# First modulation block of a hybrid NSA and mLSTM trunk: shift and scale as columns straight from the weights, with small loads and masks moved

## Chip, core and metric

The kernel is written for one core of a Trainium2 chip and runs on that core alone. Its time is device microseconds (us) from one launch; lower is better. Before the change the median of three runs is 444.39 us (444.29 to 444.74).

## What is computed

Two layers stand behind each other, each modulated by a condition vector c. The part that matters here is the modulation at the head of layer 0:

```python
for i in range(DEPTH):
    shift, scale, gate = jnp.split(c @ ada_w[i] + ada_b[i], 3, axis=-1)
    h = rmsnorm(x, norm_g[i]) * (1.0 + scale[:, None, :]) + shift[:, None, :]
    y = nsa_mixer(h, ...) if i % 2 == 0 else mlstm_mixer(h, ...)
    x = x + gate[:, None, :] * y
return rmsnorm(x, final_g)
```

x is 256 x 1024 and c is 1 x 1024, all float32. Each mixer begins with the product h @ w_in over the 1024 channels. Shift and scale of one block of 128 channels are therefore two products of c (1024) with 1024 x 128 slices of `ada_w`.

## The kernel before

**Staging.** The 1024 channels are eight blocks of 128, counted by kk. Layer 0's first phase (`first_phase`, L391) loops over kk. For each block it needs the transposed, normalized x (`xT[:, kk]`), the shift and scale columns of that block (`cols`, 128 x 2), the modulated block `hh` with its rest `hl`, and the rows of `w_in` split into a rounded part `wh` (ScalarE, L163) and a rest `wl` (VectorE, L168). Each block then takes 42 matmuls of 256 columns (`proj`, L464 to L475) into seven PSUM banks. All of layer 0 is written in the order in which it runs on every engine (`manual_schedule`, L386): each engine works through its list, and only semaphores hold it.

**Opening, in the order of the code.** SyncE issues the two halves of x and then the stream of weights (`raw`, L87): two `ada_w` slices of 512 KB for block 0, block 0's `w_in` rows, and so on. ScalarE's queue issues c, `norm_g` and part of `ada_b` into `prc` (L257 to L259). TensorE runs nine dummy matmuls on a zero tile (`warm(9)`, L266), transposes `prc` (L396), and runs six more dummies (L397). VectorE copies the result into `pca` (L399), so that column k of `pca` is block k of c, and spreads c into `crep` (L401), 32 equal columns for each block. ScalarE sums the squares of x (L410). The reciprocal root is a chain of small operations on VectorE (L209 to L213), after which x is scaled in two pieces for each half: VectorE does half 1 (L413) and ScalarE does half 0 (L414), first 128 channels and then 896. TensorE transposes xn through PSUM (L455), 16 transposes in all.

**Shift and scale of block 0.** `ada_rows` (L216 to L228) keeps `crep` stationary, 32 columns at a time in four column groups of the array, and streams the raw weights through it: 16 matmuls for the shift and 16 for the scale. What comes out are partial rows; they are copied from PSUM to SBUF (L486 on VectorE, L488 on ScalarE) and turned into columns by a product with the selector `sel` (L441). VectorE adds the biases (L445, L443), and `hh[:, 0]` follows (L493). Block 1 does its `ada_rows` among the projections of block 0, at matmul 23, copies both rows at once (L543), transposes them at matmul 33 and sums them (`ada_sums`, L1669 to L1676). Later blocks use other code.

**GpSimd** in the opening makes constants: the identity, `sel` (a memset and four rows), `int1` and `intm`, distances (`dm`, `dc`; L291 to L302), and a mask (L305 to L311). Between these stand the five DMAs of `first_small` (L478), which load parameters for the end of the first phase (`parameters`, L458).

Of the kernel before, what the change touches and what calls it, by code (L numbers as in the profile page):

```python
# [11 lines left out]
AF = mybir.ActivationFunctionType  # L12
OP = mybir.AluOpType
AX = mybir.AxisListType

P = 128
SEQ = 256
D = 1024
# [5 lines left out]
class Kernel:  # L24
# [224 lines left out]
    def setup(self):  # L249
# [6 lines left out]
        prc = self.T(self.p1, [32, P])  # L256
        nc.scalar.dma_start(prc[0:8], row(t["c"][0]))  # L257
        nc.scalar.dma_start(prc[8:16], row(t["norm_g"][0]))
        nc.scalar.dma_start(prc[16:32], row(t["ada_b"][0, 0:2048]))  # L259
        for a in range(2):  # L260
            nc.sync.dma_start(self.x[:, a], xr[:, a])
        g = nc.gpsimd

# [22 lines left out]
        self.intm = self.T(pc, [P, 8], I32)  # L286
        g.memset(self.int1, 1)
        g.memset(self.intm, 0x7FFFFFFF)

# [13 lines left out]

        m32 = self.T(self.p1, [P, P])
        g.memset(m32, 0.0)  # L305
        g.affine_select(m32, m32, pattern=[[1, P]], compare_op=OP.is_ge, fill=-1e30, base=0, channel_multiplier=-1)
# [3 lines left out]
        g.tensor_copy(self.mask, m32)  # L310
        g.tensor_copy(self.identb, self.ident)  # L311
        nc.vector.tensor_copy(self.selh, self.ident[:, 32:40])
# [3 lines left out]

        self.prc, self.pra, self.prb = prc, pra, prb

    def small_loads(self):
# [23 lines left out]
    def layer1(self):  # L343
# [11 lines left out]
        for kk in range(KC):  # L355
            if kk > 1:
                self.pairs_stream(kk)
            else:
                self.cols_stream(0, kk, P)
# [31 lines left out]
    def first_phase(self, place):  # L391
# [4 lines left out]
        nc.tensor.transpose(bt[:, 0:32], self.prc, ident[:32, :32])  # L396
        self.warm(6)  # L397
        pca = self.pca = self.T(pc, [P, 96])
# [40 lines left out]

        def column0(bank, A, cols, b):  # L440
            nc.tensor.matmul(bank[:, b : b + 1], A, self.sel[:, 0:1], start=True, stop=True, skip_group_check=True)  # L441
            if b:
                nc.vector.scalar_tensor_tensor(cols[:, 1:2], bank[:, 1:2], pca[:, 24:25], pca[:, 8:9], op0=OP.add, op1=OP.mult)  # L443
            else:
                nc.vector.tensor_tensor(cols[:, 0:1], bank[:, 0:1], pca[:, 16:17], op=OP.add)  # L445

# [3 lines left out]
        def transposed(kc, n, b):  # L450

            b = b.rearrange("p (k m) -> p k m", k=n)
            for k in range(n):
                for a in range(2):
                    nc.tensor.transpose(b[:, k, a * P : a * P + P], xn[a][:, (kc + k) * P : (kc + k) * P + P], ident)  # L455
            return xT[:, kc : kc + n], b
# [19 lines left out]

        for dst, src in self.first_small:
            nc.gpsimd.dma_start(dst, src)  # L478
        halves, raws = [self.bank(7), self.bank(3)], self.take_raw(2)
        A0 = [self.T(pc, [P, 512], tag="adaA", bufs=2)[:, :P] for _ in range(2)]  # L480
# [5 lines left out]
        nc.vector.tensor_copy(A0[0], halves[0][:, 0:P])  # L486
# [6 lines left out]
        nc.vector.tensor_scalar(self.hh[:, 0], xT[:, 0], cols[:, 1:2], cols[:, 0:1], op0=OP.mult, op1=OP.add)  # L493
        h32 = self.T(p1, [P, SEQ], tag="y32", bufs=2)
        nc.scalar.activation(h32, xT[:, 0], AF.Identity, bias=cols[:, 0:1], scale=cols[:, 1:2])
        self.make_lo(*parts)
        rest(0, h32)
        copies.append(transposed(3, 2, self.bank(5)))
        copies.append(transposed(6, 2, self.bank(7)))
        copies.append(transposed(5, 1, b6[:, SEQ:]))  # L500
        self.guests_in = True
        for n in range(2):
            nc.scalar.activation(*copies[n], AF.Copy)
        nc.vector.tensor_copy(*copies[3])
        wide = self.make_hi(place[0][1])
# [3 lines left out]
        for kk in range(KC):  # L509

            if not kk:
                self.make_lo(*wide)
            ahead = 0 < kk < KC - 1
            if ahead:
# [22 lines left out]
            for n, _ in enumerate(proj(kk)):  # L537
                if (kk, n) == (7, 8):
                    parameters()
                if not kk and n == 23:  # L540
                    bank, raws = self.bank(7), self.take_raw(2)
                    self.ada_rows(bank, raws, SEQ)
                    nc.vector.tensor_copy(A1[:, :SEQ], bank[:, :SEQ])  # L543
                if not kk and n == 33:
                    cols = self.ada_sums(A1, 9, 17, 25, 0, 7, "cols", 1)
                    modulate(1, self.hh[:, 1], cols)
                    self.make_lo(*parts)
                elif 0 < kk < KC - 1 and n == 29:
                    cols = columns(kk + 1, A)
                    modulate(kk + 1, self.hh[:, kk + 1], cols)  # L550
                    self.make_lo(*parts)
                elif (kk, n) == (KC - 1, 17):
                    self.KH, self.KL = [self.T(p1, [P, 4, 512], F32R, tag=tag) for tag in ("KH", "KL")]
                    self.dup_split((self.KH, self.KL), 0, acc[6])
                    for dst, src in self.small:
                        nc.gpsimd.dma_start(dst, src)
                    self.E, self.F = [], {}
                    self.evac_cmp(acc[4])
                    self.hi_next()
                    self.evac_cmp(acc[5], True)  # L560
                    self.lo_next()
# [118 lines left out]
    def attention(self, hidden_block):  # L680
# [46 lines left out]
        def second():  # L727
# [7 lines left out]
            nc.gpsimd.memset(W["Kc"], 0.0)  # L735
            nc.gpsimd.memset(W["Vc"], 0.0)

        def ckeys():
# [960 lines left out]
```

## Time and profile before

| | |
|---|---|
| median of three runs | 444.39 us (444.29 to 444.74) |
| profiled execution: its own time | 446.02 us |
| profiled execution: span from first to last instruction | 444.2 us |
| TensorE busy (matmuls) | 433.4 us, 98% of the span |
| VectorE, ScalarE, GpSimd busy | 337.7, 277.0, 45.0 us |
| mean DMA rate over the span | 213 GB/s |
| TensorE busy in the first 30 us | 25.69 us |
| TensorE busy from 30 to 60 us | 30.00 us |

Times in the profile count from the span's start. PE is TensorE's matmuls, PEld its weight loads, DVE is VectorE, ACT ScalarE, POOL GpSimd and SP SyncE; a letter q behind an engine means its sequencer, which issues DMAs and waits. A row of the chain of waits gives start, duration and what ran then. A row of a stage gives its length, the busy time of each engine, the granted clock of TensorE as a share of full speed, the busy share of the DMA engines, and GB/s. A row of a line or a group ends in durations in nanoseconds. A matmul's duration holds its whole way through the array; how fast such instructions follow each other is read from the chain.

### The profile page before, as it was taken

Reading aid. Unit: us, or ns where it says so; the run is one execution under the profiler, and the core shown is the slowest. Engines: PE = TensorE matmul, PEld = TensorE weight load, DVE = VectorE, ACT = ScalarE, POOL = GpSimd, SP = SyncE. Lnnn points to the kernel's source line nnn. Section 1 sums busy time; section 2 is a strip of 40 time slices with the busy share of each in tenths; the row PEclk is TensorE's granted clock in tenths of the full one; section 3 lists DMA queues with packets and bytes.
Section 4 is the critical chain, followed back from the end, with each engine's and each line's share of the span. In section 5 each row is a group of like instructions: output and inputs, shape, how many; then the busy total and the mean of one; then the engine's idle time right before and its main releaser. Section 6 shows DMA issues by size and latency. Waiting matters only on the chain.

```text
span 444.2 us, 8146 instructions
## 1 busy us (share of the span) xinstructions
PE 433.4 (98%) x2938; PEld 372.8 (84%) x2938; DVE 337.7 (76%) x771; ACT 277.0 (62%) x553; POOL 45.0 (10%) x109
## 2 busy tenths in 40 slices
PE   6999999999999999999999999999999999999994
PEld 2999999798777877788899899988888888888884
DVE  4588989888786858697996489689986978548554
ACT  4566686767896795377748686464664555465522
POOL 8000052205205020012000000000000000000000
PEclk9899999999999999999999999999999999999998
DMA  8999969892299899998999999897845899840002
GB/s 282 373 361 357 388 211 263 211 374 87 69 299 346 196 236 341 226 190 173 263 120 91 152 342 240 166 167 235 252 149 171 213 193 275 267 143 0 1 1 94
DMA packets 73688, 94.58 MB, mean 213 GB/s; under 512 B 3800, under 2 KB 51008, under 8 KB 73648
## 3 DMA queue, kind: packets, MB, share of 16 engines
q1 hardware_dynamic: 72608, 92.29, 77.5%
q0 software_dynamic: 688, 0.97, 0.8%
q10 hardware_dynamic: 352, 0.80, 0.7%
q8 instruction: 23, 0.38, 0.3%
q14 instruction: 17, 0.14, 0.1%
HBM read 93.00 MB, written 1.05 MB: 212 GB/s over the span
## 4 chain that ended last, share of the span: by engine, by line
PE 94%; DVE 2%; DMA 1%; ACT 1%; issue 1%; ACTq 0%; DVEq 0%
PE bank L604 10%; PE bank L602 9%; PE bank L603 9%; PE bank L474 8%; PE bank L1652 6%; PE bank L1651 6%; PE bank L1650 6%; PE bank L926 5%; PE bank L1561 5%; PE bank L1091 5%; PE bank L1205 4%; PE bank L225 3%; PE bank L878 3%; PE bank L861 3%; PE bank L1441 2%; PE bank L818 2%
## 5 line engine op out<-in xcount | busy, mean ns | idle before, releaser
L168 DVE TENSOR_TENSOR wl<-raw,wh 128x1024 fp32r<-128x1024 f32 (+3 forms) x126 | 137.8, 1107 | 39.8 <-ACT wh L163 38.1
L163 ACT ACTIVATE wh<-raw 128x1024 fp32r<-128x1024 f32 (+3 forms) x126 | 118.5, 963 | 61.5 <-PE bank L604 28.5
L602 PE MATMUL bank<-wh,one 128*128 128x512 f32 (+1 forms) x208 | 76.8, 370 | 0.0
L603 PE MATMUL bank<-wl,one 128*128 128x512 f32 (+1 forms) x208 | 76.3, 367 | 0.0
L604 PE MATMUL bank<-wh,one 128*128 128x512 f32 (+1 forms) x208 | 76.3, 368 | 0.0
L1650 PE MATMUL bank<-one,wh 128*128 128x256 f32 x208 | 59.5, 286 | 0.0
L1652 PE MATMUL bank<-one,wl 128*128 128x256 f32 x208 | 59.2, 285 | 0.1
L1651 PE MATMUL bank<-one,wh 128*128 128x256 f32 x208 | 59.0, 284 | 0.0
L602 PEld LDWEIGHTS bank<-wh,one 128*128 128x128 f32 x208 | 39.2, 189 | 6.1 <-DVE tz L574 0.2
L604 PEld LDWEIGHTS bank<-wh,one 128*128 128x128 f32 x208 | 39.2, 188 | 6.1
L603 PEld LDWEIGHTS bank<-wl,one 128*128 128x128 f32 x208 | 39.2, 189 | 5.9
L1652 PEld LDWEIGHTS bank<-one,wl 128*128 128x128 f32 x208 | 39.7, 191 | 0.5 <-DVE wl L168 0.3
L1651 PEld LDWEIGHTS bank<-one,wh 128*128 128x128 f32 x208 | 39.8, 191 | 0.1
L1650 PEld LDWEIGHTS bank<-one,wh 128*128 128x128 f32 x208 | 39.7, 191 | 0.1
L474 PE MATMUL bank<-one,wh 128*128 128x256 f32 x224 | 31.7, 286 | 0.3 <-ACT one L438 0.3
L842 ACT ACTIVATE Pr<-Pr,mn 128x128 f32<-128x128 f32 (+1 forms) x64 | 28.2, 447 | 1.9 <-DVE mn L835 1.6
L474 PEld LDWEIGHTS bank<-one,wh 128*128 128x128 f32 x224 | 28.5, 191 | 0.8 <-ACT one L438 0.5
L856 POOL TENSOR_SCALAR Pr<-Pr,f 128x128 f32<-128x128 f32 (+1 forms) x24 | 18.9, 800 | 49.2 <-DVE f L850 34.8
L1422 DVE SCALAR_TENSOR_TENSOR conv<-bank,one,conv 128x255 f32<-128x255 f32 (+2 forms) x48 | 20.2, 472 | 2.1 <-ACT conv L1417 2.1
L835 DVE CUSTOM_DVE_ANT_0 Pr<-bank,one 128x128 f32<-128x128 f32 (+1 forms) x64 | 18.8, 351 | 3.2 <-PE bank L821 2.1
L686 ACT ACTIVATE PT<-bank 128x384 f32<-128x384 f32 x32 | 14.6, 487 | 8.3 <-PE bank L861 8.1
L926 PE MATMUL bank<-wh,Q 128*128 128x512 f32 x48 | 16.7, 405 | 0.0
(363 smaller groups left out, 815.1 us busy)
## 6 DMA issues: line engine op xcount, KB each, us to landing
raw<-in_b_w_in SPq DMA_DIRECT2D x62, 512.0 KB, 8.4
raw<-in_ada_w SPq DMA_DIRECT2D x34, 512.0 KB, 7.3
raw<-in_b_w_out SPq DMA_DIRECT2D x16, 512.0 KB, 4.4
raw<-in_a_w_in SPq DMA_DIRECT2D x8, 512.0 KB, 7.0
raw<-in_a_cmp_w SPq DMA_DIRECT2D x8, 512.0 KB, 4.5
raw<-in_a_w_in SPq DMA_DIRECT2D x16, 256.0 KB, 4.5
raw<-in_a_w_out SPq DMA_DIRECT2D x16, 256.0 KB, 6.6
raw<-in_a_w_in SPq DMA_DIRECT2D x8, 408.0 KB, 8.4
```

The costliest lines, as they stand in the source:

```text
L163: self.nc.scalar.activation(v(hi), src, AF.Copy)
L168: self.nc.vector.tensor_sub(v(lo), src, v(hi).bitcast(F32))
L474: nc.tensor.matmul(out, w[:, ch * P : ch * P + P], h[:, kk], start=(kk == 0 and m == 0 and ch % 2 == 0), stop=(kk == 7 and m == 2), skip_g ...
L602: nc.tensor.matmul(out, self.hh[:, kk, sl], wh, start=first, stop=False, skip_group_check=True)
L603: nc.tensor.matmul(out, self.hh[:, kk, sl], wl, start=False, stop=False, skip_group_check=True)
L604: nc.tensor.matmul(out, self.hl[:, kk, sl], wh, start=False, stop=last, skip_group_check=True)
L842: nc.scalar.activation(v, v, AF.Exp, bias=mn[:, a, br, j : j + 1], scale=-1.0, accum_out=sm[:, a, br, j : j + 1])
L926: nc.tensor.matmul(out, l[:, sl], w[:, c0:c1], start=(k == 0 and m == 0), stop=(k == 7 and m == 2), skip_group_check=True)
L1091: ins = nc.tensor.matmul(out, l[:, sl], w[:, c0:c1], start=(k == 0 and m == 0), stop=(k == N - 1 and m == 2), skip_group_check=True)
L1650: nc.tensor.matmul(out, wh, self.hh[:, kk], start=first, stop=False, skip_group_check=skip)
L1651: nc.tensor.matmul(out, wh, self.hl[:, kk], start=False, stop=False, skip_group_check=skip)
L1652: nc.tensor.matmul(out, wl, self.hh[:, kk], start=False, stop=last, skip_group_check=skip)
```

## The change

Block 0's shift and scale are computed as columns at once. For each of the two, eight products of one column accumulate in PSUM: a raw 128 x 128 piece of `ada_w` is the stationary operand and column kc of `pca` is what streams. The SBUF copies and the selector products for block 0 are gone, and so are 16 + 16 matmuls with `crep`. The eight products of the shift and the first four of the scale now stand ahead of the first pair of transposes, the last four behind it. The two `ada_w` slices come in five DMAs (two halves; a half and two quarters).

Beside that: c, `norm_g` and `ada_b` are issued by SyncE behind x; six dummy matmuls become three; `sel` is made on VectorE; `int1`, `intm`, the mask and the bf16 identity are made by GpSimd in the middle of layer 0 (`late_constants`); the five DMAs of `first_small` are issued by SyncE, emitted with block 2's step; the copies of the transposes are spread differently (L503 to L506 before). For block 1, `ada_rows` moves from matmul 23 to 27, its rows are copied by two engines, and the columns come from `sel` products at matmul 34.

```diff
@@ setup
-        nc.scalar.dma_start(prc[0:8], row(t["c"][0]))
-        nc.scalar.dma_start(prc[8:16], row(t["norm_g"][0]))
-        nc.scalar.dma_start(prc[16:32], row(t["ada_b"][0, 0:2048]))
         for a in range(2):
             nc.sync.dma_start(self.x[:, a], xr[:, a])
+        nc.sync.dma_start(prc[0:8], row(t["c"][0]))
+        nc.sync.dma_start(prc[8:16], row(t["norm_g"][0]))
+        nc.sync.dma_start(prc[16:32], row(t["ada_b"][0, 0:2048]))
...
-        g.memset(self.sel, 0.0)
+        nc.vector.memset(self.sel, 0.0)
         for j in range(4):
-            g.memset(self.sel[32 * j : 32 * j + 1], 1.0)
+            nc.vector.memset(self.sel[32 * j : 32 * j + 1], 1.0)
...
+    def late_constants(self):
+        g = self.nc.gpsimd
+        g.memset(self.int1, 1)
+        g.memset(self.intm, 0x7FFFFFFF)
+        m32 = self.T(self.p1, [P, P])
+        g.memset(m32, 0.0)
+        g.affine_select(m32, m32, pattern=[[1, P]], compare_op=OP.is_ge, fill=-1e30, base=0, channel_multiplier=-1)
+        g.tensor_copy(self.mask, m32)
+        g.tensor_copy(self.identb, self.ident)
@@ layer1
+                for b, cuts in enumerate(((0, 4, 8), (0, 4, 6, 8))):
+                    self.add(None, [P, KC, P], *[((lambda v, ks=slice(*ks): v[:, ks]), ada[:, ks[0] : ks[1], D * b : D * b + P]) for ks in zip(cuts, cuts[1:])])
@@ first_phase
-        self.warm(6)
+        self.warm(3)
...
+        def direct(b, ks):
+            for kc in ks:
+                nc.tensor.matmul(ones[b][:, b : b + 1], raws[b][:, kc], pca[:, kc : kc + 1], start=(kc == 0), stop=(kc == KC - 1), skip_group_check=True)
...
-        for dst, src in self.first_small:
-            nc.gpsimd.dma_start(dst, src)
-        self.ada_rows(halves[0][:, 0:P], raws, P, (0,))
+        direct(0, range(KC))
+        direct(1, range(4))
         b6 = self.bank(6)
         nc.vector.tensor_copy(*transposed(0, 1, b6[:, 0:SEQ]))
-        nc.vector.tensor_copy(A0[0], halves[0][:, 0:P])
-        self.ada_rows(halves[1], raws, SEQ, (1,))
-        nc.scalar.activation(A0[1], halves[1][:, P:SEQ], AF.Copy)
-        copies = [transposed(1, 2, self.bank(4))]
+        direct(1, range(4, KC))
         for b in range(2):
-            column0(ones[b], A0[b], cols, b)
+            column(ones[b], cols, b, 0)
+        nc.vector.tensor_scalar(self.hh[:, 0], xT[:, 0], cols[:, 1:2], cols[:, 0:1], op0=OP.mult, op1=OP.add)
+        copies = [transposed(1, 2, self.bank(4)), transposed(3, 2, self.bank(5)), transposed(6, 2, self.bank(7)), transposed(5, 1, b6[:, SEQ:])]
+        nc.scalar.activation(*copies[0], AF.Copy)
+        nc.vector.tensor_copy(*copies[1])
...
+            if kk == 2:
+                for dst, src in self.first_small:
+                    nc.sync.dma_start(dst, src)
...
-                if not kk and n == 23:
+                if not kk and n == 27:
                     bank, raws = self.bank(7), self.take_raw(2)
                     self.ada_rows(bank, raws, SEQ)
-                    nc.vector.tensor_copy(A1[:, :SEQ], bank[:, :SEQ])
-                if not kk and n == 33:
-                    cols = self.ada_sums(A1, 9, 17, 25, 0, 7, "cols", 1)
+                    nc.vector.tensor_copy(A1[:, P:SEQ], bank[:, P:SEQ])
+                    nc.scalar.activation(A1[:, 0:P], bank[:, 0:P], AF.Copy)
+                if not kk and n == 34:
+                    cols, bank = self.T(pc, [P, 2], tag="cols", bufs=4), self.bank(7)
+                    for b in (1, 0):
+                        nc.tensor.matmul(bank[:, b : b + 1], A1[:, b * P : b * P + P], self.sel[:, 0:1], start=True, stop=True, skip_group_check=True)
```

On TensorE, between the dummies (L247) and the projections, this stood before; KH and KL are the scaled halves of x, `raw` a slice of `ada_w`, and the last pair is the selector product:

```order
L247 MATMUL bank_165<-y_9_76 128x512
L225 MATMUL bank_203<-raw_205,one_58_174 32x128 x8
L455 MATMUL bank_244<-one_20_94,KH_180 128x128
L455 MATMUL bank_244<-one_20_94,KL_181 128x128
L225 MATMUL bank_204<-raw_207,one_58_174 32x128 x8
L455 MATMUL bank_258<-one_20_94,KH_180 128x128
L455 MATMUL bank_258<-one_20_94,KL_181 128x128
L455 MATMUL bank_258<-one_20_94,KH_180 128x128
L455 MATMUL bank_258<-one_20_94,KL_181 128x128
L441 MATMUL bank_234<-one_22_99,adaA_231 128x1
L441 MATMUL bank_235<-one_22_99,adaA_232 128x1
```

and this stands there now:

```order
L247 MATMUL bank_156<-y_9_76 128x512
L449 MATMUL bank_216<-one_54_160,raw_186 128x1 x8
L449 MATMUL bank_217<-one_54_160,raw_189 128x1 x4
L465 MATMUL bank_230<-one_20_94,KH_168 128x128
L465 MATMUL bank_230<-one_20_94,KL_169 128x128
L449 MATMUL bank_217<-one_54_160,raw_189 128x1 x4
L465 MATMUL bank_241<-one_20_94,KH_168 128x128
```

Twelve one-column products (L449) are ahead of the first pair of transposes and four behind it; the other 14 transposes, of which ten stood behind the selector products, now all follow these.

On GpSimd, this stood between the distances' first part (L299) and its first operation for the end of the phase; `one_40` is `dc`, `one_16` the tile of `first_small`:

```order
L299 IOTA one_40_119 128x256 x2
L305 MEMSET one_44_147 128x128
L311 CAST one_48_153<-one_20_94 128x128
L478 DMA one_16_92<-in_a_cmp_pe 32x128
L478 DMA one_16_92<-in_norm_g 8x128
L478 DMA one_16_92<-in_ada_b 16x128
L478 DMA one_16_92<-in_a_cmp_b 1x16x4 x2
L301 TENSOR_TENSOR one_40_119<-one_40_119,one_42_120 128x256 x2
L306 AFFINE_SELECT one_44_147<-one_44_147 128x128
L302 AFFINE_SELECT one_40_119<-one_40_119 128x256 x2
L310 CAST one_46_152<-one_44_147 128x128
```

and now:

```order
L297 IOTA one_40_117 128x256 x2
L299 TENSOR_TENSOR one_40_117<-one_40_117,one_42_118 128x256 x2
L300 AFFINE_SELECT one_40_117<-one_40_117 128x256 x2
L607 CAST KH_891<-KH_891 64x2x256 x2
L607 CAST KL_892<-KL_892 64x2x256 x2
```

The mask, the casts and the DMAs are gone from between; the product and the selects of `dc` follow the iota at once. From block 1's second step on, every engine's list is the same as before, but for the five DMAs on SyncE and the late constants on GpSimd.

More of the change, by code (lines that the diff above doesn't have):

```diff
@@ L286, in setup @@
         self.intm = self.T(pc, [P, 8], I32)
-        g.memset(self.int1, 1)
-        g.memset(self.intm, 0x7FFFFFFF)
         self.dm = self.T(self.p1, [P, 4, SEQ])
@@ L302, in setup @@
             g.affine_select(self.dc[:, a].rearrange("p i g s -> p (i g) s"), self.dc[:, a].rearrange("p i g s -> p (i g) s"), pattern=[[0, 16], [-16, 16]], compare_op=OP.is_ge, fill=BIG, base=P * a - 31, channel_multiplier=1)
-        m32 = self.T(self.p1, [P, P])
-        g.memset(m32, 0.0)
-        g.affine_select(m32, m32, pattern=[[1, P]], compare_op=OP.is_ge, fill=-1e30, base=0, channel_multiplier=-1)
         self.mask = self.T(pc, [P, P], BF16)
@@ L309, in setup @@
         self.selh = self.T(pc, [P, 8], F32R)
-        g.tensor_copy(self.mask, m32)
-        g.tensor_copy(self.identb, self.ident)
         nc.vector.tensor_copy(self.selh, self.ident[:, 32:40])
@@ L357, in layer1 @@
                 self.pairs_stream(kk)
-            else:
-                self.cols_stream(0, kk, P)
+            elif kk:
+                self.cols_stream(0, kk, P)
+            else:
+                ada = t["ada_w"][0].rearrange("(k p) m -> p k m", p=P)
+                for b, cuts in enumerate(((0, 4, 8), (0, 4, 6, 8))):
+                    self.add(None, [P, KC, P], *[((lambda v, ks=slice(*ks): v[:, ks]), ada[:, ks[0] : ks[1], D * b : D * b + P]) for ks in zip(cuts, cuts[1:])])
             if kk:
@@ L438, in modulate, with column @@
             nc.scalar.activation(out, xT[:, kk], AF.Identity, bias=cols[:, 0:1], scale=cols[:, 1:2])
-        def column0(bank, A, cols, b):
-            nc.tensor.matmul(bank[:, b : b + 1], A, self.sel[:, 0:1], start=True, stop=True, skip_group_check=True)
+        def direct(b, ks):
+            for kc in ks:
+                nc.tensor.matmul(ones[b][:, b : b + 1], raws[b][:, kc], pca[:, kc : kc + 1], start=(kc == 0), stop=(kc == KC - 1), skip_group_check=True)
+        def column(bank, cols, b, kk):
             if b:
-                nc.vector.scalar_tensor_tensor(cols[:, 1:2], bank[:, 1:2], pca[:, 24:25], pca[:, 8:9], op0=OP.add, op1=OP.mult)
+                nc.vector.scalar_tensor_tensor(cols[:, 1:2], bank[:, 1:2], pca[:, 24 + kk : 25 + kk], pca[:, 8 + kk : 9 + kk], op0=OP.add, op1=OP.mult)
             else:
-                nc.vector.tensor_tensor(cols[:, 0:1], bank[:, 0:1], pca[:, 16:17], op=OP.add)
+                nc.vector.tensor_tensor(cols[:, 0:1], bank[:, 0:1], pca[:, 16 + kk : 17 + kk], op=OP.add)
         def rest(kk, h32):
@@ L475, in proj @@
                     yield
-        for dst, src in self.first_small:
-            nc.gpsimd.dma_start(dst, src)
-        halves, raws = [self.bank(7), self.bank(3)], self.take_raw(2)
-        A0 = [self.T(pc, [P, 512], tag="adaA", bufs=2)[:, :P] for _ in range(2)]
+        raws = self.take_raw(2)
         cols = self.T(pc, [P, 2], tag="cols", bufs=4)
         ones = [self.bank(2 - b) for b in range(2)]
-        self.ada_rows(halves[0][:, 0:P], raws, P, (0,))
+        direct(0, range(KC))
+        direct(1, range(4))
         b6 = self.bank(6)
         nc.vector.tensor_copy(*transposed(0, 1, b6[:, 0:SEQ]))
-        nc.vector.tensor_copy(A0[0], halves[0][:, 0:P])
-        self.ada_rows(halves[1], raws, SEQ, (1,))
-        nc.scalar.activation(A0[1], halves[1][:, P:SEQ], AF.Copy)
-        copies = [transposed(1, 2, self.bank(4))]
+        direct(1, range(4, KC))
         for b in range(2):
-            column0(ones[b], A0[b], cols, b)
+            column(ones[b], cols, b, 0)
[3 more added lines that the diff above has]
+        nc.vector.tensor_copy(*copies[1])
         parts = self.make_hi(place[0][0])
-        nc.vector.tensor_scalar(self.hh[:, 0], xT[:, 0], cols[:, 1:2], cols[:, 0:1], op0=OP.mult, op1=OP.add)
+        self.make_lo(*parts)
         h32 = self.T(p1, [P, SEQ], tag="y32", bufs=2)
         nc.scalar.activation(h32, xT[:, 0], AF.Identity, bias=cols[:, 0:1], scale=cols[:, 1:2])
-        self.make_lo(*parts)
         rest(0, h32)
-        copies.append(transposed(3, 2, self.bank(5)))
-        copies.append(transposed(6, 2, self.bank(7)))
-        copies.append(transposed(5, 1, b6[:, SEQ:]))
+        nc.vector.tensor_copy(*copies[3])
         self.guests_in = True
-        for n in range(2):
-            nc.scalar.activation(*copies[n], AF.Copy)
-        nc.vector.tensor_copy(*copies[3])
         wide = self.make_hi(place[0][1])
@@ L539, in first_phase @@
                     parameters()
-                if not kk and n == 23:
+                if not kk and n == 27:
                     bank, raws = self.bank(7), self.take_raw(2)
                     self.ada_rows(bank, raws, SEQ)
-                    nc.vector.tensor_copy(A1[:, :SEQ], bank[:, :SEQ])
-                if not kk and n == 33:
-                    cols = self.ada_sums(A1, 9, 17, 25, 0, 7, "cols", 1)
+                    nc.vector.tensor_copy(A1[:, P:SEQ], bank[:, P:SEQ])
[4 more added lines that the diff above has]
+                        nc.tensor.matmul(bank[:, b : b + 1], A1[:, b * P : b * P + P], self.sel[:, 0:1], start=True, stop=True, skip_group_check=True)
+                    for b in (1, 0):
+                        column(bank, cols, b, 1)
                     modulate(1, self.hh[:, 1], cols)
@@ L736, in second @@
             nc.gpsimd.memset(W["Vc"], 0.0)
+            self.late_constants()
         def ckeys():
```

## Prediction

> **What bounds the kernel now.** I read the page first, then who waited for whom on TensorE, then the chain of waits and stages of the opening.
>
> ```profile
> span 444.2 us, 8146 instructions
> PE 433.4 (98%) x2938; PEld 372.8 (84%) x2938; DVE 337.7 (76%) x771; ACT 277.0 (62%) x553; POOL 45.0 (10%) x109
> ...
> PE bank L247 <- DVE y L265: 1.2, 1, 1.2
> PE bank L396 <- DMA one<-in_ada_b: 1.2, 1, 1.2
> PE bank L455 <- ACT KH L414: 1.1, 1, 1.1
> PE bank L455 <- DVE KL L413: 0.5, 1, 0.5
> PE bank L474 <- ACT one L438: 0.3, 1, 0.3
> ```
>
> TensorE is the bound, and these five are all the waits of its matmuls that the view lists; all lie ahead of 21.6 us. After that TensorE stays full, so the question is only when the first projection (L474) starts and how much TensorE work the first block carries: a microsecond gained there should be kept to the end. The stages of the opening, in whole windows of the granted clock (columns: length, PE, PEld, DVE, ACT, POOL busy, clock, DMA share, GB/s):
>
> ```profile
> 4.40:7.81 3.41, 2.18 (x17) 0.82 (x19) 1.50 (x7) 2.58 (x5) 3.39 (x9) 1.00 1.12 325
> 7.81:11.23 3.42, 1.86 (x35) 1.08 (x28) 3.35 (x6) 1.42 (x3) 2.46 (x6) 0.97 1.07 356
> 11.23:14.64 3.41, 3.41 (x19) 3.41 (x19) 2.03 (x7) 2.82 (x7) 0.00 (x0) 0.53 1.15 369
> 14.64:18.05 3.41, 3.41 (x43) 3.28 (x45) 1.65 (x4) 2.25 (x3) 0.00 (x0) 1.00 1.08 368
> ```
>
> The clock is halved for one window of 3.41 us, right behind a window in which TensorE was busy 1.86 us (54%); the window with 2.18 us (64%) had no such effect. The chain through the opening:
>
> ```profile
> 5.96 0.23 PE bank L396
> ...
> 7.67 0.66 DVE rq_a L212
> ...
> 8.36 0.55 DVE rq_y L213
> ...
> 8.93 1.19 DVE KL L413
> ...
> 10.17 0.33 PE bank L455
> ...
> 12.10 0.65 PE bank L441 x4
> 12.75 2.04 PE bank L455 x10
> 14.79 2.86 PE bank L474 x24
> ...
> 20.06 0.23 PE bank L1669 x2
> ...
> 21.56 3.96 PE bank L474 x30
> 25.52 0.79 PE bank L431 x8
> ```
>
> The first projection starts in this row:
>
> ```profile
> 14.55 0.36 PE L474 MATMUL bank<-one,wh 128*128 128x256 f32 x1
> ```
>
> **Part 1: GpSimd out of VectorE's way.** The three DVE steps of this chain are too long for what they do. Here is L212 with its other two calls, what GpSimd ran meanwhile, and a row of like size:
>
> ```profile
> L212 DVE SCALAR_TENSOR_TENSOR rq_a<-rq_a,rq_v x3: 160/161/650, 7.7 to 195.3; 128x1 f32<-128x1 f32 x2, 128x2 f32<-128x2 f32 x1
> ...
> 4.89 0.68 POOL L478 DMA_DIRECT2D one<-in_a_cmp_pe  x1
> ...
> 7.67 1.21 POOL L301 TENSOR_TENSOR one<-one,one 128x256 f32<-128x256 f32 x2
> ...
> 9.07 0.96 POOL L302 TENSOR_SCALAR_AFFINE_SELECT one<-one 128x256 f32<-128x256 f32 x2
> ...
> L486 DVE COPY adaA<-bank 128x128 f32<-128x128 f32 x1 | 0.3, 273 | 0.0
> ```
>
> L212 takes 0.65 us exactly while L301 runs, and 0.16 later in the program; L213 (0.55) and L413's first piece (1.19) lie under the rest of GpSimd's list. With the DMAs (from 4.89 on) and the mask gone from between, L301 and L302 follow the iota and need 1.21 + 0.96 = 2.2 us from about 4.9: over by 7.1, ahead of L212. I take 0.16 for L212 and L213 and 0.27 for L413's piece (L486, same size). The root is then ready at 7.67 + 0.16 + 0.16 = about 8.0, the first piece of xn at 8.3, and ScalarE's, which starts with it, not much later, where the pair of transposes used to run at 9.4 and 10.17. Bounds: nothing, if the long steps have another cause; the full 1.8 us, if nothing else is late. What is late next is TensorE's own list, part 2.
>
> **Part 2: sixteen one-column products.** The trace has the same kind of product, a 128 x 128 stationary block against one column: each is two passes (L431: four products, x8). At full clock a pass costs 0.79 / 8 = 0.099 us, at the halved clock 0.65 / 4 = 0.163 (L441). Sixteen products are 32 passes: 3.2 us at full clock, 5.2 at half. Their weights are raw tiles instead of `adaA`; the shape is the same, so I take 0.099. What lets them start are `pca`, the dummies and the weights:
>
> ```profile
> 0.73 0.86 SPq L261 DMA_DIRECT2D one<-in_x  x2
> ...
> 1.64 1.06 SPq L87 DMA_DIRECT2D raw<-in_ada_w  x2
> ...
> 1.66 4.16 DMA one<-in_ada_b
> ...
> one<-in_x SPq DMA_DIRECT2D x1, 512.0 KB, 4.4
> ...
> raw<-in_ada_w SPq DMA_DIRECT2D x1, 512.0 KB, 5.8
> ...
> raw<-in_ada_w SPq DMA_DIRECT2D x1, 512.0 KB, 7.1
> ...
> one<-in_a_cmp_pe POOLq DMA_DIRECT2D x1, 16.0 KB, 4.6
> ...
> 6.10 1.47 PE L247 MATMUL bank<-y 128*128 128x512 bf16 x6
> ```
>
> The second half of x was issued at about 1.2 and landed 4.4 later, at 5.6; `ada_b` landed at 5.82 though it is 8 KB: it stood beside x. Behind x on one queue it can hardly land before 5.6, so I leave L396 at 5.96. At the other end, small loads on GpSimd's queue took 4.6 us; issued behind x by 2.7 (three issues of about 0.5 us, as those of `ada_w`, the last from 2.7), they would land at 7.3. Three dummies end at 6.10 + 0.75 = 6.85, by when `pca` (0.45 behind L396) is there. The two slices landed at 1.64 + 5.8 = 7.4 and 2.1 + 7.1 = 9.2, 1.8 us apart; by that rate the first half lands at 6.6, the rest of the first slice at 7.4, the half and two quarters of the second at 8.3, 8.8 and 9.2. That the issues are up to 2 us later on SyncE costs nothing, as the DMA engines are busy all along (share 1.12): what is issued waits behind x. So the twelve products run from 6.85 to 6.85 + 24 x 0.099 = 9.2, the pair of transposes to 9.45 (0.23 for two, L1669), the last four products to 10.25. No piece is late for its product by these numbers, the last by 0.2 at most.
>
> From there two paths meet. TensorE: 14 transposes at 0.115, to 11.85. ScalarE and VectorE:
>
> ```profile
> L503 ACT ACTIVATE xT<-bank 128x512 f32<-128x512 f32 x2 | 1.1, 582 | 0.0
> ...
> L163 ACT ACTIVATE wh<-raw 128x512 fp32r<-128x512 f32 x2 | 1.1, 620 | 0.0
> ...
> L493 DVE TENSOR_SCALAR one<-xT,cols 128x256 fp32r<-128x256 f32 x1 | 0.4, 414 | 0.0
> L443 DVE SCALAR_TENSOR_TENSOR cols<-bank,one 128x1 f32<-128x1 f32 x1 | 0.2, 220 | 0.3 <-PE bank L441 0.3
> ```
>
> VectorE has the columns and `hh` by 10.25 + 0.3 + 0.22 + 0.41 = 11.2. ScalarE now copies a bank of xT ahead of `wh`: four transposes end at 10.7, the copy runs from 11.0 to 11.6, the first half of `wh` to 12.2. The first projection thus starts at **12.2 instead of 14.55: 2.35 us**. The SBUF copies (L486, L488) that left the path are in this sum; `sel` on VectorE lies where it waits for its first data.
>
> **Part 3: block 1 and the rest.** Two `sel` products are four passes, 0.40 us, for two transposes of 0.23: 0.17 more on a full TensorE. Its wait for block 1's `hh` (0.3) changes little: seven matmuls (0.85 us) lie behind the products, against about 0.3 + 0.22 + 0.60 of columns and modulation. I count nothing for it. The late constants run on GpSimd, which is busy 10%; they can block VectorE for what they last, about 1 us in sum, where TensorE has its own backlog: 0, at worst 0.5. The five small DMAs on SyncE stand in the middle of the stream of weights and delay its issues by some 2 us, which waits of landed tiles cover; at worst one stall of that size, which I give no room.
>
> **Sum.** 2.35 - 0.17 = 2.2 us. The profiled execution takes 446.02 us for a span of 444.2; it is 1.6 above the median, which I put down to profiling. Against its own time the sum gives a span of 442.0 and 443.8 us, against the median **442.2 us**.
>
> **Rivals.** *The clock halves as before, from 11.23 to 14.64.* The Trainium skill ("TensorE: Matmul & The Clock Gate", Why this matters for your kernels) puts the drop behind idle gaps of over about 3 us; by that no window here would fall, and the forecast stands. The trace speaks against it: the longest wait behind the start was 1.2 us, and the clock still went to 0.53. Whether 32 passes of one column count as work is what no row shows. If they don't, 8.5 transposes are done by 11.23, 5.5 more take 0.204 each (2.04 / 10), projections start at 12.35 at 0.24 each (twice 2.86 / 24), and 9.6 are done at 14.64 where one was: 8.6 x 0.119 - 0.17 = 0.85 us gained, **443.5**.
>
> *The small loads land late*, at 7.3 instead of 5.8. Everything behind them moves by 1.5 us; 0.7 is left with the full clock, and with a halved one from 11.23, 14 transposes cost 1.2 more, so -0.5. I take no change, **444.3**.
>
> *The clock falls a window sooner*, at 7.81, as three dummies fewer leave the stage 4.40:7.81 with about 0.4 + 0.75 us of wide work and a pass or ten. Then 22 passes and a pair run at half: 22 x 0.204 + 0.41 puts the last product at 12.8, nine transposes are done by 14.64, and projections start at 15.25: 0.7 + 0.17 slower, 445.3. If products and transposes don't bring the clock back, either, it stays at half to 18.05: projections from 15.7, 10 done in that time where 3.4 us of work were, **446.8**. The Trainium skill, same page ("Part 4: PE-mode transpose"), says that transposes don't count as busy for the clock; by that it would be 446.8. The trace disagrees: the stage 11.23:14.64 held 13 of them, and the clock was back at 14.64. It decides at 7.81: half the dummies, against products that do or don't count. For it speaks the thin margin between 54% and 64% above.
>
> **Chances.** Forecast 0.47, the halved clock as before 0.22, late loads 0.13, the earlier fall 0.18. The range, 441.5 to 444.6, holds the first three: below the forecast lie 0.3 for the wait at block 1 and 0.4 for x or the loads coming sooner. A measurement can tell 0.2%, 0.9 us, from no change. Faster by that are the forecast and a third of the halved clock: 0.55. Slower is the earlier fall less the part of it that stays near 445.2: 0.12. The rest, 0.33, is no change.
>
> **What would show it.** Right: L212 and L213 at 0.16 and L413's first piece under 0.4; one-column passes 0.1 apart from 6.9 on; the first projection at 12.2; clock 1.00 throughout; block 1's first matmul 2 us sooner than 21.56, and the same lead at the end. The forecast is wrong if the clock rows show 0.5 ahead of 11.23, if the first product waits for `pca` beyond 7, if the stream of weights makes ScalarE wait in blocks 1 and 2, or if a lead at 21 us is lost later.

## The result and the profile after

The change makes the kernel slower: **448.69 us, the median of ten executions (446.93 to 450.31), against 444.57 us (444.10 to 447.51, ten) before; ratio 1.0087, 95% interval 1.0064 to 1.0110.** The forecast was 442.2, with a range to 444.6. Its third rival, the clock that falls and is not brought back by products and transposes, had said 446.8; in the trace below the clock does not fall, it is at half from the start to 20.21 us.

The page of the profile after (450.12 us for a span of 448.3), whose counterpart of before stands at the head of the prediction:

```profile
span 448.3 us, 8137 instructions
PE 439.8 (98%) x2933; PEld 379.9 (85%) x2933; DVE 336.5 (75%) x775; ACT 276.4 (62%) x552; POOL 41.7 (9%) x99
```

TensorE has five matmul records fewer and is busy 6.4 us longer. Who waited for whom on TensorE lists two waits where there were five:

```profile
PE bank L247 <- DVE y L265: 1.2, 1, 1.2
PE bank L403 <- DMA one<-in_ada_b: 0.6, 1, 0.6
```

So the time was not lost in waiting; TensorE did its work more slowly. The order of time on VectorE (start, duration) shows that the first part of the forecast came as worked out:

```profile
7.19 0.16 DVE L212 SCALAR_TENSOR_TENSOR rq_a<-rq_a,rq_v 128x2 f32<-128x2 f32 x1
7.38 0.16 DVE L213 SCALAR_TENSOR_TENSOR rq_y<-rq_a,rq_y 128x2 f32<-128x2 f32 x1
7.58 0.88 DVE L420 TENSOR_SCALAR KL<-one,rq_y 128x128 f32<-128x128 f32 x2
```

The chain of waits through the opening shows where it went wrong (L449 is the one-column products, L465 the transposes, L484 the projections, L438 block 1's later columns):

```profile
5.85 0.28 PE bank L403
6.13 1.39 PE bank L247 x3
7.52 4.91 PE bank L449 x24
...
12.96 1.50 PE bank L449 x8
14.46 0.97 PE bank L465 x4
...
25.56 3.96 PE bank L484 x30
29.53 0.79 PE bank L438 x8
```

Three dummies take 1.39 us, 0.46 each, and 24 passes take 4.91, 0.205 each: twice what the same work costs at the end of this piece, where eight passes take 0.79. Block 1 starts at 25.56 instead of 21.56, 4.0 of the 4.1 us by which the span grew (448.3 for 444.2). The stages, cut at the clock's own steps (length, PE, PEld, DVE, ACT, POOL busy, clock, DMA share, GB/s):

```profile
13.38:16.80 3.42, 3.42 (x18) 3.42 (x18) 1.24 (x5) 1.35 (x3) 0.00 (x0) 1.00 1.06 385
16.80:20.21 3.41, 3.41 (x18) 3.41 (x17) 2.93 (x6) 2.93 (x5) 0.00 (x0) 1.00 1.11 386
20.21:23.62 3.41, 3.41 (x52) 3.08 (x52) 0.29 (x1) 0.10 (x1) 0.00 (x0) 1.00 1.12 356
```

Here the clock column misleads: the record of the clock begins with its first change, at 20.21, and what lies ahead of that is shown as 1.00. The starts of the instructions tell the truth: the dummies of this trace follow each other every 0.427 us and its transposes every 0.213, where at full clock dummies follow each other every 0.215 us (the profile before, from 6.33 on) and transposes every 0.11 (the repeated before, below). (The 18 matmuls of a window ahead of 20.21 and the 52 behind it are no measure, since 32 of the 52 are the small matmuls of `ada_rows`, four side by side.) TensorE was busy for all of the first two windows, at half clock.

### The profile page after: what moved, and what is told of

It is laid out like the page before. It is cut to its first block, busy times and chain, and to the rows that moved or that the text cites. A ratio compares the mean times of both kernels' runs of the same rounds, so it can differ in the third digit from the quotient of the medians.

```text
span 448.3 us, 8137 instructions
## 1 busy us (share of the span) xinstructions
PE 439.8 (98%) x2933; PEld 379.9 (85%) x2933; DVE 336.5 (75%) x775; ACT 276.4 (62%) x552; POOL 41.7 (9%) x99
## 4 chain that ended last, share of the span: by engine, by line
PE 93%; DMA 2%; ACT 1%; DVE 1%; SPq 1%; issue 1%; DVEq 0%; ACTq 0%
PE bank L615 9%; PE bank L613 9%; PE bank L614 9%; PE bank L484 7%; PE bank L1664 6%; PE bank L1663 6%; PE bank L1662 5%; PE bank L938 5%; PE bank L1573 5%; PE bank L1103 5%; PE bank L1217 4%; PE bank L890 3%; PE bank L873 3%; PE bank L225 2%; PE bank L1453 2%; PE bank L830 2%
## 5 line engine op out<-in xcount | busy, mean ns | idle before, releaser
L1664 PE MATMUL bank<-one,wl 128*128 128x256 f32 x208 | 59.2, 285 | 0.1
L484 PE MATMUL bank<-one,wh 128*128 128x256 f32 x224 | 32.6, 291 | 0.1
L484 PEld LDWEIGHTS bank<-one,wh 128*128 128x128 f32 x224 | 29.3, 196 | 0.6 <-ACT one L445 0.3
L484 PE MATMUL bank<-one,wl 128*128 128x256 f32 x112 | 17.0, 291 | 0.0
```

The lines of the kernel that those rows point to most:

```text
L484: nc.tensor.matmul(out, w[:, ch * P : ch * P + P], h[:, kk], start=(kk == 0 and m == 0 and ch % 2 == 0), stop=(kk == 7 and m == 2), skip_g ...
L1664: nc.tensor.matmul(out, wl, self.hh[:, kk], start=False, stop=last, skip_group_check=skip)
```

## The experiments

Three theories stood at first. **A**: products of one column are no work for the clock gate, so they keep the clock at half. **B**: it is the three dummies that were taken out. **C**: it is the moves (small loads behind x, masks later). A fourth, **D**, came out of the first eight runs. Each run is compared with the kernel before, timed beside it: its median was 444.54 us beside the first four runs below, 444.60 beside the next four, 444.40 beside the last four. A ratio weighs the executions of both kernels; it is not that of the two medians, and differs from it by up to 0.5%.

**The kernel before, once more.** No edit.

> The kernel before, unchanged, to see how much its own executions differ in the clock. Theory A (one-column products are no work for the clock gate): 444.1 to 445.0 us again, the clock raised by the first nine dummies in most executions. If the gate's windows run free of the program, the first change of the clock lies at another time than 4.2 us, by up to 3.4 us, and the time moves by under 1 us. Rival B (the dummies are what counts): the same.

444.42 us (444.04 to 447.96; ratio 1.0002, 0.9983 to 1.0021). Its chain differs from the profile that I worked from:

```profile
10.16 0.33 PE bank L455
...
11.99 1.15 PE bank L455 x10
13.14 2.87 PE bank L474 x24
...
19.92 3.96 PE bank L474 x30
```

Projections start at 13.14, not 14.79, and block 1 at 19.92, not 21.56. The clock was full from 5.46 on. The profiled execution of before, at 446.02, was one with a halved window of 3.4 us that most executions do not have: of these twelve, nine (444.04 to 445.03) have a mean granted clock of 0.995 to 0.997, two (446.02, 446.26) have the 0.993 of that profile, and one (447.96) has 0.990; its own time was not inflated by profiling, for here too it is the span and 1.8 us (444.42 for 442.6).

**The moves alone.** Before, with the small loads behind x, `sel` on VectorE, the masks made late and `first_small` on SyncE:

```diff
-        nc.scalar.dma_start(prc[0:8], row(t["c"][0]))
...
+        nc.sync.dma_start(prc[0:8], row(t["c"][0]))
...
-        g.memset(self.sel, 0.0)
+        nc.vector.memset(self.sel, 0.0)
...
-        g.tensor_copy(self.mask, m32)
-        g.tensor_copy(self.identb, self.ident)
...
-            nc.gpsimd.dma_start(dst, src)
+            if kk == 2:
+                for dst, src in self.first_small:
+                    nc.sync.dma_start(dst, src)
+            self.late_constants()
```

> Only the moves: small loads behind x, GpSimd's list shortened, late constants, first_small on SyncE; block 0 by ada_rows and six dummies as before. Theory A: nothing is lost, and VectorE's root is ready 1.5 us sooner: 442.5 to 444.0 us. Rival C (the moves themselves cost, by late small loads or by SyncE's issues): 446 to 449 us. Rival B: as A.

444.34 us (ratio 0.9992, 0.9981 to 1.0004): C is out. Block 1 starts at 18.57, 1.35 us sooner than in the repeated before, yet the span is only 0.25 shorter. In the chain the lead meets ScalarE, which makes `adaA` for later blocks (L424, whose weights landed at 19.18) ahead of block 1's second `wh`:

```profile
12.25 6.92 DMA Q<-in_ada_w
...
19.26 0.91 ACT adaA L424 x2
...
20.66 0.74 ACT wh L163
...
21.45 1.94 PE bank L476 x14
```

TensorE waits 0.7 us there, a wait that before does not have: part of a lead in the opening is given back to the stream of weights. Of the 1.35 us, 0.49 are left at block 2 (24.17 instead of 24.66).

**The products alone.** Before, with block 0's products of one column, the five DMAs and the new order of the copies; six dummies, GpSimd's list and block 1 as before.

```diff
...
-        self.ada_rows(halves[0][:, 0:P], raws, P, (0,))
+        direct(0, range(KC))
+        direct(1, range(4))
...
```

> Only block 0's one-column products, with six dummies, GpSimd's list, queues and block 1 as before. Theory A: the passes run at 0.21 us and the clock is at half until the projections are well on: 447 to 450 us. Rival B (three dummies too few): full clock, a pass in 0.10 us, 443 to 445 us. Rival C: 444 to 445 us.

451.22 us (448.04 to 451.44, six executions, two of them under 449; ratio 1.0122, 1.0095 to 1.0150):

```profile
6.17 2.67 PE bank L247 x6
8.84 4.91 PE bank L446 x24
...
14.29 1.50 PE bank L446 x8
```

In this trace the passes still take 0.205 each, with all six dummies. The products alone carry the loss, and more than all of it.

**Thirty-two columns instead of one.** After, with each product streaming 32 equal columns of `crep`. The arguments of its matmul:

```diff
-  ones[b][:, b : b + 1], raws[b][:, kc], pca[:, kc : kc + 1]
+  ones[b][:, 0:32], raws[b][:, kc], self.crep[:, kc]
```

> The changed kernel with each product streaming 32 equal columns (crep) instead of one, the same weights. Theory A, if columns that stream are what counts: somewhat more work for the gate, but 32 columns fill only a quarter of a pass: between 444 and 449 us. If weight loads alone set the pass and count for nothing: 448 to 449 us, unchanged. Rivals B and C: 448 to 449 us, unchanged.

448.99 us (448.75 to 450.37, five executions; ratio 1.0096, 1.0077 to 1.0115), `7.62 4.96` for the 24 passes: a pass costs the same for 32 columns as for one, and the time was no better. In the trace the clock rose at 16.80, one window sooner than in after's.

**Six dummies again.** After, with `self.warm(6)`.

> After with six dummy matmuls of 512 columns in place of three, nothing else. Theory A (one-column products are no work for the clock): the dummies add work to the stage ahead of the products only, the passes still run 0.21 us apart, clock raised at 17 us or later, time 448.5 to 451.5 (three dummies at half clock are 1.3 us more). Rival B (the three dummies that were taken out kept the clock up): clock full from about 5 to 8 us, passes 0.10 apart, time 442.5 to 445.

446.07 us (444.84 to 451.17; ratio 1.0051, 1.0024 to 1.0078), and in groups: one execution at 444.84, eight at 445.7 to 446.2, one at 447.84, two at 451. The profiled one is the fastest, with the clock full from 5.76 on:

```profile
6.42 1.40 PE bank L247 x6
7.83 2.57 PE bank L449 x24
...
10.68 0.79 PE bank L449 x8
```

Neither A nor B stands as told: two executions at 451 had all six dummies, and here 32 passes ran at 0.099 to 0.107 without pulling the clock down. But the three dummies bring back 2.6 of the 4.1 us at the median (446.07 instead of 448.69), so that taking them out is part of the loss.

**A hundred and twenty-eight columns.** After, with each product streaming 128 equal columns. The arguments of its matmul:

```diff
-  ones[b][:, b : b + 1], raws[b][:, kc], pca[:, kc : kc + 1]
+  ones[b][:, 0:P], raws[b][:, kc], pca[:, kc : kc + 1].to_broadcast([P, P])
```

> After with each of the sixteen products streaming 128 equal columns instead of one; the first column is used, as in after. If the clock counts how long columns stream (theory A in its narrow form: 32 columns raised it one window earlier, 16.8 instead of 20.2): raised within one or two windows of the first product, by 13.4 at the latest, and 445 to 447.5. If it is the kind of product (float32 in two passes, a weight load for each) that does not count, however wide: clock raised at 16.8 or later, time 448.5 to 450.

445.19 us (ratio 1.0007, 0.9991 to 1.0023), in two groups of six: 443.98 to 444.48 and 445.91 to 446.61. No execution above 447 is left, and all twelve have a mean granted clock of 0.995 or more, so that none was pulled down once it had risen. The profiled one (444.24) had the clock raised at 3.89, ahead of any product, so it does not show the products raising it.

**A dummy behind each product.** After, with one line in the loop of `direct`:

```diff
+                self.warm(1)
```

> After with one dummy matmul of 512 bf16 columns behind each of the sixteen one-column products (16 x 0.21 us at full clock, 16 x 0.43 at half). Theory A: more than half of TensorE's time is then wide work, the clock is full from 10 us at the latest, passes 0.10 apart, and the opening costs about 16 x (0.20 + 0.21) = 6.6 us where it was 6.4 in after, but transposes and projections run at full speed: 445 to 447, faster than after. If something else holds the clock down (the moves, the loads' traffic), it stays at half to 17 us or more, the dummies cost 16 x 0.43 = 6.9 us, and the time is over 452.

452.78 us (447.33 to 452.85; ratio 1.0134, 1.0089 to 1.0178), four of six executions at 452.8 and two at 447.3 to 447.6: a miss for A as I had it. A piece of its chain:

```profile
16.15 0.22 PE bank L449 x2
16.37 0.45 PE bank L247
16.82 0.22 PE bank L449 x2
```

A dummy takes 0.45 of each 0.67 us, so two thirds of the time is wide work; the clock still rose only at 20.55. The time is the one that I had written for another cause than the products; the moves were ruled out as a loss by their own run (444.34), and theory D below accounts for it by a share that is still too small.

**All but the products.** After, with block 0's rows, copies and selector products of before, and six dummies; each `ada_w` slice of block 0 comes in one DMA again.

> The complement: after with block 0's shift and scale made by before's rows, copies and selector products, with six dummies and before's order of the copies; the loads behind x, the masks made later, sel on VectorE and block 1's new place stay. Theory A: clock full from about 5.7, first projection near 11.5 to 12, time 443.5 to 444.6, with block 1's change worth 0.3 us at most either way. If block 1's change or the moves carry part of the loss: over 445.

444.29 us (443.55 to 444.89; ratio 0.9981, 0.9966 to 0.9997): the rest of the change, with block 1's part in it, is no loss, and a gain of 0.1 to 0.2% (0.1% by the medians, 444.29 against 444.60).

**Theory D.** Set side by side, the traces show a clock that changes only on a grid of 3.41 us whose place differs between executions. The nine dummies of the start run from 1.19, 0.427 apart at half clock, to 5.00, which is longer than a window but shorter than two. What share of a window they fill depends on where the grid lies:

| trace | window | share with columns streaming | clock at its end |
|---|---|---|---|
| before | 0.81 to 4.22 | 0.89 | raised |
| before, again | 2.05 to 5.46 | 0.87 | raised |
| 128 columns | 0.48 to 3.89 | 0.79 | raised |
| six dummies | 2.35 to 5.76 | 0.78 | raised |
| products alone | 0.33 to 3.74 | 0.75 | half |
| dummy behind each | 6.90 to 10.31 | 0.68 | half |
| after | 3.15 to 6.56 | 0.69 | half |
| after | 13.38 to 16.80 | 0.72 | half |
| 32 columns | 13.39 to 16.80 | 0.76 | raised |

(Windows are counted back in steps of 3.41 from a recorded change. A share is the time of dummies, 0.427 us each, and of transposes, 0.213 each, by their starts in the trace; a pass of one column counts as nothing, one of 32 as 0.05 us.) Before's window from 11.05 to 14.46, which raised the clock, comes to 0.77 by this reckoning and fits; the expectation below has it as 0.74. The limit lies near three quarters and no finer, since 0.75 did not raise the clock and 0.76 did. By D a busy TensorE whose columns do not stream is idle for the clock; the products miss the raise when the dummies missed it, and drop the clock when a window holds little else. It was tested by filling the first wait: eleven dummies ahead of L403 instead of nine, so that they run on to 5.7 or later and, with those behind L403, fill over three quarters of some window wherever the grid lies.

```diff
-        self.warm(9)
+        self.warm(11)
```

**After, with eleven dummies.**

> After with eleven dummies ahead of the wait for the small loads instead of nine (1.19 to 5.9 us at half clock instead of 5.06), the three behind it kept. Theory D, made from the ten traces so far: the clock is decided at the end of each window of 3.41 us, whose place differs between executions; it goes up when columns streamed for over about 0.75 of the window (0.78 to 0.90 raised it, 0.72 and less did not, 0.74 and 0.76 were seen both ways), and is kept down to about 0.4 (0.39 kept it); a one-column product streams for nothing. By D nearly every execution is now raised by 6.8, so the slowest group (449 to 450.3, never raised ahead of 16) is gone; windows filled by products still drop it in some executions: groups near 444.3 and 446 to 447, median under 446.8. Theory A as I had it (products hold the clock at half whatever is ahead): 448 to 450 as in after.

447.10 us (445.10 to 448.90; ratio 1.0041, 1.0017 to 1.0064): four executions at 445.1 to 445.5, six at 446.9 to 447.4, two at 448.7 to 448.9. The group at 450 is gone; the median is 0.3 above what I had written, and no execution reaches the 444.3 that I had expected for some. The mean granted clock is 0.993 to 0.994 in the first group, 0.989 to 0.991 in the second and 0.986 to 0.987 in the third, where executions without a halved window have 0.995 or more. So the clock was pulled down in all twelve; the traced one (0.989) was at half for two windows, which makes it about one, two and three windows by group, with some 1.7 us from group to group. The profiled execution (446.93) shows the fall that I had only inferred. Its windows and its chain:

```profile
1.86:5.27 3.41, 3.41 (x9) 1.21 (x8) 1.00 (x5) 1.51 (x4) 3.41 (x17) 1.00 0.99 353
5.27:8.69 3.42, 3.18 (x24) 2.44 (x23) 2.13 (x10) 2.49 (x5) 0.12 (x1) 1.00 1.17 323
8.69:12.10 3.41, 3.41 (x19) 3.41 (x19) 0.49 (x2) 0.29 (x1) 0.00 (x0) 0.50 1.07 369
12.10:15.51 3.41, 3.41 (x18) 3.41 (x18) 2.12 (x5) 2.34 (x5) 0.00 (x0) 0.50 1.09 394
```

```profile
6.19 0.75 PE bank L247 x3
6.94 3.21 PE bank L449 x24
...
10.68 1.50 PE bank L449 x8
12.18 3.09 PE bank L465 x14
```

Raised at 5.27 (only the record's first entry; the 1.00 of the row ahead of it is the same blank as in after), it fell at 8.69, behind a window in which TensorE was busy 3.18 of 3.42 us. About 0.3 of that window were dummies, the rest passes. The next window held one pair of transposes and passes, and the clock stayed at half; the third was full of transposes, and it rose at 15.51.

**The same with 128 columns.** The only difference from the run above is how many columns a product streams.

> The same eleven dummies, with the products streaming 128 equal columns, the first of which is used. Theory D: raised by 6.8 in nearly every execution and never dropped, since the products now stream all along: one group, 443.9 to 444.6, and the group at 446 that nine dummies left is gone. If products in float32 lower the clock whatever they stream, a second group at 446 stays.

444.42 us, all twelve executions within 444.24 to 444.62 (ratio 0.998, 0.996 to 1.000), with a mean granted clock of 0.995 to 0.998: none was pulled down. The group at 446 is gone, as D said:

```profile
6.47 0.75 PE bank L247 x3
7.23 2.68 PE bank L449 x24
9.90 0.22 PE bank L465 x2
10.12 0.89 PE bank L449 x8
...
12.66 3.66 PE bank L484 x28
...
19.76 3.96 PE bank L484 x30
```

A pass of 128 columns takes 0.112 us, hardly more than one of one column, and it keeps the clock. This is nearly the change as I forecast it, with the clock full from 5.78 on (the passes take 3.57 us where one column took 3.36 in the run with six dummies), and it is no faster than before.

**Rows, with eleven dummies.** All of the change but the products, as above.

> The version with block 0's rows as before and all else as in after, with eleven dummies ahead. Theory D: raised early in every execution, no fall: 443.5 to 444.3 with a smaller spread than nine dummies gave (443.55 to 444.89). If the spread has another cause than the clock (transfers), it stays 1.3 us wide.

443.96 us (443.65 to 445.06; ratio 0.9975, 0.9953 to 0.9996): the best of all, faster than before by 0.25% by the ratio and 0.1% by the medians (444.40 beside it; five of its 35 executions lie above 447 and weigh in the ratio). The spread did not shrink as D said (1.4 us, 1.3 with nine dummies), so it has another cause than this one. Its chain:

```profile
9.41 0.64 PE bank L225 x16
...
12.14 3.35 PE bank L487 x28
...
18.99 3.96 PE bank L487 x30
```

**Before, with five dummies.**

```diff
-        self.warm(9)
+        self.warm(5)
```

> Before with five dummies ahead of the small loads instead of nine: no one-column products for block 0, no moved loads. Theory D: five dummies stream 2.1 us, 0.63 of a window at most, so the clock is not raised ahead of the six dummies behind the small loads, in many executions not ahead of the transposes; the opening runs at half clock and the time is 446.5 to 450, as slow as after. If it is only the one-column products that lower the clock (theory A): 444.2 to 445.

444.63 us (444.25 to 446.76; ratio 0.9996, 0.9973 to 1.0019), a miss for D as I had used it, and the time that I had written for A. The clock rose at 9.93 in its trace:

```profile
6.17 2.69 PE bank L247 x6
...
8.90 1.08 PE bank L225 x16
...
13.14 2.87 PE bank L474 x24
```

Six dummies (2.69 us at half clock) and sixteen matmuls of the rows, whose 128 columns do stream, filled 0.77 of the window from 6.51 on by the reckoning above: before has a second chance to raise the clock that the change removed. And the half clock up to 9.93 cost nothing, since the projections still start at 13.14: the dummies and the first rows lie ahead of a wait for xn. By this trace the miss was in what I let the rows count and in the cover, not in the rule.

## Why the prediction was wrong, point by point

**GpSimd out of VectorE's way: right.** L212 and L213 take 0.16 us each at 7.19 and 7.38, where 0.65 and 0.55 stood; both pieces of xn take 0.88 together. They are as short with the moves alone and as long as before with the products alone. But in the changed kernel the pieces wait for TensorE, whose products come first: with 128 columns and a full clock xn is begun at 7.93 and the first transposes run at 9.90.

**Small loads behind x: right.** L403 starts at 5.85, L396 started at 5.96; the rival that had them at 7.3 is false.

**Sixteen products at 0.099 us a pass, the step that failed.** The forecast took the full clock for them because the dummies ahead were at full clock in the profile of before. In after's trace the clock was at half from the start; 24 passes took 4.91 us instead of 2.4, the last product ended at 14.46 instead of 10.25, and the projections began at 17.2 instead of 12.2. Runs with the clock up gave 2.57 us for the 24 passes: the price was nearly right for that clock (0.107 a pass with six dummies, 0.112 with eleven). The price at half clock, 0.163 from a row of four passes and 0.204 from transposes in the rival, was 0.205 to 0.213. (In that rival the last product comes out at 12.7 by its own terms, not 12.8.)

**The clock.** I had read the halved window of before by TensorE's busy share, 54% against 64% (the clock's own steps there are 7.64 and 11.05, 0.2 ahead of my rows, which hardly changes the share), and put the question of whether passes of one column count into two rivals, at 0.22 (443.5) and 0.18 (part of it at 446.8). By theory D they do not: a window busy 3.18 of 3.42 us dropped the clock in the run with eleven dummies, where a window busy 2.96 of 3.41 us kept it with six dummies behind L403:

```profile
5.76:9.17 3.41, 2.96 (x22) 2.33 (x22) 2.13 (x10) 2.38 (x5) 0.00 (x0) 1.00 1.15 326
```

What shows it is the pair of runs that differ in the columns alone: with one column all twelve executions lost windows, with 128 none did. By the rule of the Trainium skill ("TensorE: Matmul & The Clock Gate", Why this matters for your kernels), which puts a drop behind idle gaps, the forecast would have stood, and the runs speak against it: with eleven dummies TensorE waited 1.2 us at the longest, and the clock fell. The window of the Trainium skill (same page, Part 1: The HAM clock gate), which it says runs freely and does not start with the kernel, agrees with the steps of 3.41 us and with groups of times for one and the same kernel. In the same rival I had let transposes count as doubtful; they count (the window from 12.10 in the run with eleven dummies), as I had said against the Trainium skill (same page, Part 4: PE-mode transpose).

**Against which time.** I subtracted 2.35 us, measured from a first projection at 14.55, from a median of executions in which it starts at 13.14 by the chain where the profiled one has 14.79. So 1.65 us of the forecast gain was the halved window of one execution, and no gain for the median. That its 1.6 us above the median were profiling was wrong: every profiled execution here takes its span and 1.8 us.

**Block 1: 0.17 was enough.** From the record of the first projection to block 1 there are 7.02 us in the repeated before (12.90 to 19.92) and 7.10 with 128 columns and full clock (12.66 to 19.76): 0.08 more, where I counted 0.17. (The 13.14 of the chain is the end of the transposes, 0.24 behind that first record, and can't be set against 12.66, where a projection had waited for `wh`.)

**"Kept to the end": in part.** The forecast let a lead at the first projection reach the end. In the traces, a lead at block 1 over the repeated before of 1.35 us (the moves alone) left 0.25 in the span, one of 0.16 (128 columns, eleven dummies) nothing, and one of 1.15 (all but the products, nine dummies ahead, 18.77) left 0.9.

**The sum.** From 442.2 to 448.69 are 6.5 us: 1.65 for the unlucky baseline; 0.55 that was left of the 2.2 and did not come (444.42 with the clock held against 444.40 before; the first projection starts at 12.66 there, where I had 12.2 and the repeated before has 12.90; block 1 starts 0.16 sooner, and the spans are equal); 4.3 for the clock (448.69 against 444.42, between which lie the dummies and the wider products). What the change saves in copies and selector products it pays in passes, 3.57 us (2.68 + 0.89) against about 1.3 for 32 matmuls of the rows (twice 0.64), half of which lie under the wait for xn.

**What stays open.** How low a share drops the clock is known from two sides only: 0.3 dropped it with eleven dummies, and so did about 0.35 in before's window from 7.64 to 11.05 (0.9 us of rows and three transposes), while nearly 0.4 (six dummies in the traced run, 1.31 of 3.41 us by columns) kept it. By what mechanism the chip tells streaming from loading, no run shows. D is a rule that fits the traces: it foretold the run with eleven dummies and 128 columns, came within 0.3 us for one column, and missed the time of before with five dummies. That the six executions of after at a mean granted clock of 0.986 to 0.990 were raised early and dropped, like the traced one at 0.989 with eleven dummies, while the other four (0.996 to 0.998) were never raised ahead of the projections, is inferred from those means; one of the four is traced.

## What to carry to other kernels

Ask of a busy TensorE how much of it streams columns: work that mostly loads weights can cost twice over, once in its own passes and once in all that runs at the lower clock behind it, and widening it to columns that nobody needs can cost next to nothing. Before a forecast is set against a median, compare the profiled execution with the other times; one that lies outside their range carries an event of its own, and a gain that removes that event is not there in the others. Give the first dummies of a kernel enough length to fill well over three quarters of some clock window wherever the grid lies (here eleven, 4.7 us, with three more behind the wait); up to the first wait for data they cost nothing.

## What the runs showed that I had not expected

A float32 product of a 128 x 128 stationary block takes 0.10 to 0.11 us a pass at full clock for 1 or 128 columns, and 0.205 to 0.213 at half for 1 or 32. The clock column of a stage reads 1.00 for all that lies ahead of the first recorded change, even where dummies run 0.43 apart. One kernel's executions fall into groups up to 6.3 us apart (444.84 to 451.17) in the same runs. Between the two traced executions of before, the clock's grid lies 1.24 us apart (changes at 4.22 and 5.46), and only one has a halved window.
